# A two-layer trunk on one core: norm sums from one tile of squares, turned tiles split straight out of PSUM, and the last halves scaled and stored by two engines

## The chip, the cores and the metric

The kernel runs on one core of a Trainium2 chip. The metric is the device time of one execution in microseconds, the median over several runs. The engines are named as in the profile: PE (TensorE, matmul), PEld (its weight load), DVE (VectorE), ACT (ScalarE), POOL (GpSimd) and SP (SyncE, which here only issues DMAs).

## What is computed

The reference is a decoder trunk of two layers over 512 tokens of width 1024, in float32. Layer 0 mixes with a gated convolution and a pooling over several window sizes, layer 1 with a gated position mixing; each layer then has a gated feed-forward net of hidden width 2816, and a norm closes the trunk.

```python
def rms_norm(x, g):
    y = x * rsqrt(mean(x * x, axis=-1) + EPS)
    return y * g

def reference(x, ...):
    h = x
    # layer 0
    proj = rms_norm(h, norm_mix[0]) @ w_in_even          # a_b, a_c, a_v, z_b: 512 columns each
    y_a = a_b * causal_dwconv3(a_c * a_v, conv_a)
    y_b = multiscale_pool(z_b, w_pool, pool_scale)       # windows 2, 4, 8, 16
    h = h + concat(y_a, y_b) @ w_out_even
    h = h + gated_conv_ffn(rms_norm(h, norm_ffn[0]), ...)
    # layer 1
    ...                                                  # mixer C
    h = h + gated_conv_ffn(rms_norm(h, norm_ffn[1]), ...)
    return rms_norm(h, final_norm)
```

## The kernel before

**Layout.** The residual `h` lies in SBUF with the features on the partitions: eight tiles `h[k]` of 128 features by 512 tokens. A product in float32 is made of three fast matmuls: each operand is split into a high part, rounded to the fast format, and a low part that holds the rest (`hi` and `lo`), and `mm3` adds hi x hi (L139), lo x hi (L140) and hi x lo (L141) into one PSUM bank. So each tile of weights and of activations passes through ScalarE, which writes `hi`, and VectorE, which subtracts it from the raw value to get `lo`. For weights `parts` does this (`whi` at L134, `wlo` at L135).

**The norm** is not applied to the activations ahead of a product. The products use `h` times the gain, split into `hgh` and `hgl`, and the results are scaled by the reciprocal root of each token's mean square later. Class `Norm` collects the squares: ScalarE squares `h[k]`, GpSimd adds the squares into one tile `ssq` (L195). With `apart=True`, which norms m0 (first mixer), f0 and f1 (the two feed-forward nets) use, the eighth square is not added but kept in a tile `last`. `rstd_tokens` then sums over the partitions on TensorE, with two matmuls of one column for each of four tiles of tokens, one on `ssq` (L203) and one on `last` (L204): eight in all, into `sst`. `inv_sqrt_cols` makes the reciprocal root out of it with a square root on ScalarE (L233) and one Newton step in small VectorE operations; `rstd_spread` turns the result into a tile over all tokens (`ssr`, L211, and a copy at L214).

**The z stage** opens the kernel. `x` comes with the tokens on the partitions, so for each k TensorE turns four 128 x 128 blocks into a PSUM bank `xt_ps` (L363). From there, in `turn(k)`:

```python
inorder(nc.scalar.activation(whi, wraw, AF.Copy))                      # L371
inorder(nc.vector.tensor_copy(h[k], ps))                               # L372
inorder(nc.scalar.activation(hg[k][0], h[k], AF.Copy, scale=g))        # L374
inorder(nc.vector.tensor_tensor(wlo, wraw, ..., ALU.subtract))         # L375
inorder(nc.vector.scalar_tensor_tensor(hg[k][1], h[k], g, hg[k][0]))   # L376
norm.square(k, inorder)                                                # L188, L191, L194
```

`turn(k + 1)` is called when the group `z` begins its products of k. `in_group("z", ...)` then adds 12 matmuls of 128 x 512 per k into four banks. At the end of its first bank `z_done` starts the norm's sums, at the third it spreads the root and starts the pooling of VectorE (`z_pool`).

**Behind it** follow the groups `ac`, `av`, the pooled product (its weights `wpl` are split by two instructions at the end of the z stage's code) and `ab`, each with four splits of weights of 128 x 1024, and then the output projection. The raw weights come through one SP queue with four buffers; `whi` and `wlo` have six.

**Order.** A scheduler places the instructions of each engine by priorities and estimated times. `inorder` keeps marked instructions in the order of the program among themselves; `behind(a, b)` puts instruction a after b in the order, without a semaphore.

**The feed-forward nets** begin with `direct`, which calls `first(i, j)` ahead of each product of three matmuls; at `(1, 0)` it calls `rstd_tokens`, at `(2, 2)` `rstd_spread`.

**The end.** The last product of the second net is finished for four tiles of tokens, each in two halves of 512 columns: VectorE adds the residual, ScalarE squares with a running sum, `newton` gives the root's parts, and VectorE scales both halves (L950) with two factors at once, `r` and `ms`; SP stores each half (L952).

Of the kernel before, what the change touches and what calls it, by code (L numbers as in the profile page):

```python
# [8 lines left out]
F32 = mybir.dt.float32  # L9
# [6 lines left out]
P = 128  # L16
D = 1024
S = 512
# [12 lines left out]
def tile_trunk(ctx: ExitStack, tc: tile.TileContext, x, norm_mix, norm_ffn, final_norm,  # L31
# [96 lines left out]
        nc.scalar.activation(hi, raw, AF.Copy)  # L128
        return hi, lo

    def parts(raw, a, b, name):
        hi = wp.tile([P, a, b], F32R, tag="whi", bufs=6, name=f"whi_{name}")
        lo = wp.tile([P, a, b], F32R, tag="wlo", bufs=6, name=f"wlo_{name}")
        nc.scalar.activation(hi, raw, AF.Copy)  # L134
        nc.vector.tensor_tensor(lo, raw, hi.bitcast(F32), ALU.subtract)  # L135
        return hi, lo

    def mm3(ps, lhs, rhs, start, stop):
# [33 lines left out]
    class Norm:  # L172


        def __init__(self, name, gain, apart=False):
            self.name, self.gain, self.n, self.apart = name, gain, 0, apart
            self.ssq = tp.tile([P, S], F32, tag="ssq", bufs=1, name=f"ssq_{name}")

        def add(self, k):
# [3 lines left out]
                                           op0=ALU.mult, op1=ALU.subtract)  # L183
            self.square(k)

        def square(self, k, order=lambda ins: ins):
            if self.n == 0:
                order(nc.scalar.activation(self.ssq, h[k], AF.Square))  # L188
            elif self.n == NK - 1 and self.apart:
                self.last = tp.tile([P, S], F32, tag="rstd", name=f"last_{self.name}")  # L190
                order(nc.scalar.activation(self.last, h[k], AF.Square))  # L191
            else:
                sq = tp.tile([P, S], F32, tag="sq", name=f"sq_{self.name}{k}")
                order(nc.scalar.activation(sq, h[k], AF.Square))  # L194
                nc.gpsimd.tensor_tensor(self.ssq, self.ssq, sq, ALU.add)  # L195
            self.n += 1

        def rstd_tokens(self):

            ps = aux_bank(f"sst_{self.name}")  # L200
            for t in range(NT):
                ts_ = slice(t * P, (t + 1) * P)
                nc.tensor.matmul(ps[:, t : t + 1], self.ssq[:, ts_], ones, start=True, stop=False)  # L203
                nc.tensor.matmul(ps[:, t : t + 1], self.last[:, ts_], ones, start=False, stop=True)  # L204
            self.cols = inv_sqrt_cols(ps[:, :NT], NT, f"{self.name}t")

        def rstd_spread(self):

            ps = aux_bank(f"ssr_{self.name}")
            for t in range(NT):  # L210
                nc.tensor.transpose(ps[:, t * P : (t + 1) * P],  # L211
                                    self.cols[:, t : t + 1].to_broadcast([P, P]), ident)
# [4 lines left out]
        def rstd_cols(self):  # L217
            ps = aux_bank(f"ssc_{self.name}")
            for t in range(NT):
                nc.tensor.matmul(ps[:, t : t + 1], self.ssq[:, t * P : (t + 1) * P],  # L220
                                 ones, start=True, stop=True)
            return inv_sqrt_cols(ps[:, :NT], NT, f"{self.name}c")

    def work(key, n, name):
        if n == S:
# [86 lines left out]
    def in_parts(chunks, k, raw):  # L312
        hi, lo = parts(*raw)
        for i in range(raw[1]):
            chunks[k + i] = hi[:, i, :], lo[:, i, :]

    def in_group(name, w, c0, lhs_is_weight, on_done, tail, chunks=None, before=None):
        if chunks is None:
            chunks = {}
            for k in range(0, NK, 2):  # L320
                in_parts(chunks, k, in_fetch(name, w, c0, k, 2))
# [12 lines left out]
        if lhs_is_weight:  # L334
            group(name, range(4), list(range(NK)), wt, lambda k, j: hg_k(k), tail, on_done, before)
        else:
            group(name, range(4), list(range(NK)), tokens, wt_wide, tail, on_done, before)

    def mixer0():
        nonlocal prm0  # L340
        w = w_in_even[0]
        with tc.tile_pool(name="m0", bufs=1) as mp:
            prm_mix = params("mix", [("mix", rows_of(norm_mix[0]), NK)], nc.scalar)
            norm = Norm("m0", lambda k: prm_mix("mix", k), apart=True)
            zchunks = {}
            xt = {}

# [6 lines left out]
                raws[k] = in_fetch("z", w, 1536, k, n)  # L354

            raws = {}
            for k, n in ((0, 1), (1, 1), (2, 2), (4, 2)):
                load(k, n)

            def turn(k):  # L360
                ps = mm_bank(f"xt_ps{k}")
                for t in range(NT):
                    nc.tensor.transpose(ps[:, t * P : (t + 1) * P], xt[k][:, t, :], ident)  # L363
# [7 lines left out]
                inorder(nc.scalar.activation(whi, wraw, AF.Copy))  # L371
                inorder(nc.vector.tensor_copy(h[k], ps))  # L372
                g = prm_mix("mix", k)
                inorder(nc.scalar.activation(hg[k][0], h[k], AF.Copy, scale=g))  # L374
                inorder(nc.vector.tensor_tensor(wlo, wraw, whi.bitcast(F32), ALU.subtract))  # L375
                inorder(nc.vector.scalar_tensor_tensor(  # L376
                    hg[k][1], h[k], g, hg[k][0].bitcast(F32), op0=ALU.mult, op1=ALU.subtract))
                norm.square(k, inorder)
                if k == 0:
                    load(6, 2)  # L380

# [16 lines left out]

            def z_done(g, ps):
                if g == 0:  # L400
                    norm.rstd_tokens()
# [70 lines left out]

            in_group("ab", w, 0, True, b_done, 4)

            nxt = Norm("f0", lambda k: prm0("ffn", k), apart=True)
            project("oe", w_out_even[0], mix, [4, 5, 6, 7, 0, 1, 2, 3], nxt)
            return nxt

# [15 lines left out]
    class Ffn:  # L494
# [262 lines left out]
    def mixer1(norm):  # L757
        w = w_in_odd[0]
        with tc.tile_pool(name="m1", bufs=1) as mp:
# [113 lines left out]
                    for j in ((4,), (5,), (6, 7))[k - 1]:  # L873
                        turned(j)

            nxt = Norm("f1", lambda k: prm1("ffn", k), apart=True)
            project("oo", w_out_odd[0], mix, list(range(NK)), nxt, before=second_half)
            return nxt

# [1 line left out]
    def ffn1(norm):  # L881
        with tc.tile_pool(name="f1", bufs=1) as ap:
# [20 lines left out]
            for groups, a, b in PARTS:  # L903
# [24 lines left out]
                def done(j, ps):  # L928
# [18 lines left out]
                    nc.vector.tensor_scalar(ms, ms, 1.5, None, op0=ALU.add)  # L947
                    for c in range(2):
                        cs = slice(c * 512, (c + 1) * 512)
                        nc.vector.tensor_scalar(y[t][:, cs], yf[c], r, ms,  # L950
                                                op0=ALU.mult, op1=ALU.mult)
# [50 lines left out]
```

## Time and profile before

| | us |
|---|---|
| median of three runs | 1000.65 (1000.1 to 1001.06) |
| the profiled execution | 1000.02 |
| its span on the core | 998.3 |
| TensorE busy | 986.5 (99%) |
| VectorE, ScalarE, GpSimd busy | 699.9, 522.7, 100.6 |

The mean clock that TensorE was granted is 0.998. Rows of the timeline that are shown below read: start in us from the span's start, duration in us, engine, line, operation, output <- inputs, their shapes, how many instructions the row joins, and in brackets the engine's idle time before it with what ended it. Successive records of one engine overlap by up to a tenth of a microsecond. Rows of the waits read: engine, waiting output and line, what it waited for, and then total us, count and the longest.

### The profile page before, as it was taken

The page shows a single profiled execution, that of the slowest core. Times are in us where ns is not written, and L with a number is a line of the kernel's source. Part 1 is how long each engine was busy: PE and PEld are TensorE (multiplying, and loading weights), DVE is VectorE, ACT ScalarE, POOL GpSimd, SP SyncE. Part 2 cuts the span into 40 slices and gives each one's busy share as a digit, 9 for nine tenths or more (in the row PEclk, how much of TensorE's full clock was granted, in tenths as well). Part 3 has the DMA queues.
Part 4 walks back from the last instruction along what each step waited for, and adds up shares of the span by engine and source line. Part 5 has one row for each costly group of instructions (what it writes and reads, how often), then busy time and mean ns, then how long its engine had stood idle before and what let it go on. Part 6 is the DMA issues. An engine that isn't in the chain of part 4 may idle for free.

```text
span 998.3 us, 14727 instructions
## 1 busy us (share of the span) xinstructions
PE 986.5 (99%) x5835; PEld 874.5 (88%) x5835; DVE 699.9 (70%) x1057; ACT 522.7 (52%) x775; POOL 100.6 (10%) x117
## 2 busy tenths in 40 slices
PE   8999999999999999999999999999999999999997
PEld 6888888898999989999888888888989899898995
DVE  5977457967785877858943645389668868688677
ACT  6522345744653746537655444675536366363663
POOL 3032030300000000000300001202000010000100
PEclk9999999999999999999999999999999999999999
DMA  7532225454554645546433223434535446354442
GB/s 233 184 105 85 85 85 127 107 150 124 130 145 106 175 121 132 144 106 184 132 127 106 63 86 104 100 91 118 158 95 145 141 112 184 94 141 146 119 115 84
DMA packets 81904, 124.53 MB, mean 125 GB/s; under 512 B 4292, under 2 KB 53676, under 8 KB 81836
## 3 DMA queue, kind: packets, MB, share of 16 engines
q1 hardware_dynamic: 73580, 98.96, 31.6%
q0 software_dynamic: 6912, 23.07, 12.9%
q10 hardware_dynamic: 1344, 1.58, 0.5%
q8 instruction: 45, 0.74, 0.3%
q14 instruction: 23, 0.19, 0.1%
HBM read 98.42 MB, written 2.10 MB: 101 GB/s over the span
## 4 chain that ended last, share of the span: by engine, by line
PE 92%; DVE 4%; DMA 2%; ACT 1%; issue 0%; SPq 0%; POOL 0%; DVEq 0%; ACTq 0%; POOLq 0%
PE d L139 4%; PE d L140 4%; PE d L141 4%; PE dn L139 4%; PE dn L140 3%; PE dn L141 3%; PE gu L139 3%; PE gu L141 3%; PE gu L140 3%; PE u L141 1%; PE oo L141 1%; PE oo L139 1%; PE u L140 1%; PE u L139 1%; PE oe L140 1%; PE oe L139 1%
## 5 line engine op out<-in xcount | busy, mean ns | idle before, releaser
L139 PE MATMUL dn<-whi_dn,a_hi 128*128 128x512 f32 x176 | 68.7, 390 | 0.0
L140 PE MATMUL d<-a_lo,whi_d 128*128 128x512 f32 x176 | 68.6, 390 | 0.0
L140 PE MATMUL dn<-wlo_dn,a_hi 128*128 128x512 f32 x176 | 68.6, 390 | 0.0
L141 PE MATMUL d<-a_hi,wlo_d 128*128 128x512 f32 x176 | 68.5, 389 | 0.0
L514 DVE SCALAR_TENSOR_TENSOR c<-rows,prm,c 128x512 f32<-128x512 f32 x88 | 67.5, 791 | 0.0
L141 PE MATMUL dn<-whi_dn,a_lo 128*128 128x512 f32 x176 | 67.3, 390 | 0.0
L139 PE MATMUL d<-a_hi,whi_d 128*128 128x512 f32 x176 | 66.9, 390 | 0.0
L127 POOL DMA_DIRECT2D wlo_g<-raw_g x22 | 19.1, 868 | 382.3 <-ACT wlo_g L126 350.7
L931 DVE TENSOR_TENSOR y<-dn,y 128x512 f32<-128x512 f32 x48 | 32.3, 685 | 22.8 <-PE dn L141 22.3
L126 ACT ACTIVATE wlo_g<-raw_g 128x1024 fp32r<-128x1024 f32 x22 | 23.2, 1055 | 42.4 <-PE dn L140 42.4
L135 DVE TENSOR_TENSOR wlo_u<-raw_u,whi_u 128x1024 fp32r<-128x1024 f32 x16 | 19.6, 1223 | 34.2 <-ACT whi_u L134 34.1
L520 ACT ACTIVATE s<-c,prm 128x512 f32<-128x512 f32 x44 | 30.9, 717 | 22.7 <-DVE c L514 22.6
L640 ACT ACTIVATE whi_s12u<-s12u 128x1024 fp32r<-128x1024 f32 x18 | 18.9, 1050 | 43.1 <-PE d L140 33.7
L641 DVE TENSOR_TENSOR wlo_s34u<-s34u,whi_s34u 128x1024 fp32r<-128x1024 f32 x18 | 22.1, 1226 | 26.1 <-ACT whi_s34u L640 26.1
L141 PEld LDWEIGHTS dn<-whi_dn,a_lo 128*128 128x128 f32 x176 | 33.0, 188 | 7.5 <-DVE a_lo L255 0.2
L140 PEld LDWEIGHTS d<-a_lo,whi_d 128*128 128x128 f32 x176 | 33.1, 188 | 7.2 <-DVE a_lo L255 0.2
L139 PEld LDWEIGHTS dn<-whi_dn,a_hi 128*128 128x128 f32 x176 | 33.1, 188 | 7.1 <-ACT a_hi L253 0.2
L139 PEld LDWEIGHTS d<-a_hi,whi_d 128*128 128x128 f32 x176 | 32.8, 188 | 7.0
L298 DVE TENSOR_TENSOR h<-d,h 128x512 f32<-128x512 f32 x48 | 32.5, 685 | 9.2 <-PE d L141 9.2
L141 PEld LDWEIGHTS d<-a_hi,wlo_d 128*128 128x128 f32 x176 | 33.0, 188 | 6.7
L140 PEld LDWEIGHTS dn<-wlo_dn,a_hi 128*128 128x128 f32 x176 | 33.1, 188 | 6.5
L135 DVE TENSOR_TENSOR wlo_dn<-raw_dn,whi_dn 128x1024 fp32r<-128x1024 f32 x22 | 26.8, 1221 | 12.8 <-ACT whi_dn L134 12.8
(1201 smaller groups left out, 3412.3 us busy)
## 6 DMA issues: line engine op xcount, KB each, us to landing
raw_g<-in_w_ffn_gate_dram SPq DMA_DIRECT2D x36, 512.0 KB, 4.0
raw_u<-in_w_ffn_up_dram SPq DMA_DIRECT2D x36, 512.0 KB, 4.0
wlo_g<-raw_g POOLq DMA_DIRECT2D x22, 512.0 KB, 4.8
raw_d<-in_w_ffn_down_dram SPq DMA_DIRECT2D x22, 512.0 KB, 4.4
raw_dn<-in_w_ffn_down_dram SPq DMA_DIRECT2D x22, 512.0 KB, 4.7
wlo_u<-raw_u POOLq DMA_DIRECT2D x18, 512.0 KB, 4.7
raw_oe<-in_w_out_even_dram SPq DMA_DIRECT2D x8, 512.0 KB, 3.5
raw_g<-in_w_ffn_gate_dram SPq DMA_DIRECT2D x16, 256.0 KB, 2.9
```

The lines of the kernel that those rows point to most:

```text
L126: nc.scalar.activation(lo, raw, AF.Copy, scale=-1.0)
L127: nc.gpsimd.dma_start(lo, raw, accum_op=ALU.add)
L135: nc.vector.tensor_tensor(lo, raw, hi.bitcast(F32), ALU.subtract)
L139: nc.tensor.matmul(ps, lhs[0], rhs[0], start=start, stop=False)
L140: nc.tensor.matmul(ps, lhs[0], rhs[1], start=False, stop=False)
L141: nc.tensor.matmul(ps, lhs[1], rhs[0], start=False, stop=stop)
L298: nc.vector.tensor_tensor(h[k], ps, h[k], ALU.add)
L514: nc.vector.scalar_tensor_tensor(c, t[:, i : S + i], prm("cf", i * NF + ft), c, op0=ALU.mult, op1=ALU.add)
L520: nc.scalar.activation(s, c, AF.Silu, bias=self.prm("bf", ft))
L640: nc.scalar.activation(hi, src, AF.Copy)
L641: nc.vector.tensor_tensor(lo, src, hi.bitcast(F32), ALU.subtract)
L931: nc.vector.tensor_tensor(dst, ps, dst, ALU.add)
```

## The change

- **Norm.** `apart` and `rstd_tokens` are gone. All eight squares go into `ssq` by way of GpSimd, and `rstd_cols` sums it with four matmuls of one column (`ssc`). In the feed-forward nets it is called at `(1, 2)`, the spread at `(2, 1)`, both kept in the order of the program.
- **z stage.** `hgh`, `hgl` and the square read the turned tile in PSUM; `h[k]` is still copied, after `hgl`. VectorE's order for a k is wlo, hgl, copy. The splits of `wpl` and of the four `ac` weights are put behind the last square (ScalarE) and the last hgl (VectorE) of the stage.
- **End.** The Newton step is written out so that one factor `r` comes out; VectorE scales the low half and SP stores it, ScalarE scales the high half and stores it through its own queue.

```diff
-    def parts(raw, a, b, name):
+    def parts(raw, a, b, name, after=(None, None)):
...
-        nc.scalar.activation(hi, raw, AF.Copy)
-        nc.vector.tensor_tensor(lo, raw, hi.bitcast(F32), ALU.subtract)
+        behind(nc.scalar.activation(hi, raw, AF.Copy), after[1])
+        behind(nc.vector.tensor_tensor(lo, raw, hi.bitcast(F32), ALU.subtract), after[0])
...
-        def square(self, k, order=lambda ins: ins):
+        def square(self, k, order=lambda ins: ins, src=None):
+            src = h[k] if src is None else src
             if self.n == 0:
-                order(nc.scalar.activation(self.ssq, h[k], AF.Square))
-            elif self.n == NK - 1 and self.apart:
-                self.last = tp.tile([P, S], F32, tag="rstd", name=f"last_{self.name}")
-                order(nc.scalar.activation(self.last, h[k], AF.Square))
+                order(nc.scalar.activation(self.ssq, src, AF.Square))
             else:
...
-        def rstd_tokens(self):
-            ps = aux_bank(f"sst_{self.name}")
-            for t in range(NT):
-                ts_ = slice(t * P, (t + 1) * P)
-                nc.tensor.matmul(ps[:, t : t + 1], self.ssq[:, ts_], ones, start=True, stop=False)
-                nc.tensor.matmul(ps[:, t : t + 1], self.last[:, ts_], ones, start=False, stop=True)
-            self.cols = inv_sqrt_cols(ps[:, :NT], NT, f"{self.name}t")
...
+        def rstd_cols(self, order=lambda ins: ins):
             ps = aux_bank(f"ssc_{self.name}")
             for t in range(NT):
-                nc.tensor.matmul(ps[:, t : t + 1], self.ssq[:, t * P : (t + 1) * P],
-                                 ones, start=True, stop=True)
-            return inv_sqrt_cols(ps[:, :NT], NT, f"{self.name}c")
+                order(nc.tensor.matmul(ps[:, t : t + 1], self.ssq[:, t * P : (t + 1) * P],
+                                       ones, start=True, stop=True))
+            self.cols = inv_sqrt_cols(ps[:, :NT], NT, f"{self.name}c")
+            return self.cols
...
+            fed = [None, None]
+            def put_square(ins):
+                fed[1] = inorder(ins)
...
                 inorder(nc.scalar.activation(whi, wraw, AF.Copy))
+                g = prm_mix("mix", k)
+                inorder(nc.scalar.activation(hg[k][0], ps, AF.Copy, scale=g))
+                inorder(nc.vector.tensor_tensor(wlo, wraw, whi.bitcast(F32), ALU.subtract))
+                fed[0] = inorder(nc.vector.scalar_tensor_tensor(
+                    hg[k][1], ps, g, hg[k][0].bitcast(F32), op0=ALU.mult, op1=ALU.subtract))
                 inorder(nc.vector.tensor_copy(h[k], ps))
-                g = prm_mix("mix", k)
-                inorder(nc.scalar.activation(hg[k][0], h[k], AF.Copy, scale=g))
-                inorder(nc.vector.tensor_tensor(wlo, wraw, whi.bitcast(F32), ALU.subtract))
-                inorder(nc.vector.scalar_tensor_tensor(
-                    hg[k][1], h[k], g, hg[k][0].bitcast(F32), op0=ALU.mult, op1=ALU.subtract))
-                norm.square(k, inorder)
+                norm.square(k, put_square, ps)
...
-            nc.scalar.activation(wpl_hi, wpl, AF.Copy)
-            nc.vector.tensor_tensor(wpl_lo, wpl, wpl_hi.bitcast(F32), ALU.subtract)
+            behind(nc.scalar.activation(wpl_hi, wpl, AF.Copy), fed[1])
+            behind(nc.vector.tensor_tensor(wpl_lo, wpl, wpl_hi.bitcast(F32), ALU.subtract), fed[0])
...
-            in_group("ac", w, 512, True, c_done, 4)
+            in_group("ac", w, 512, True, c_done, 4, after=fed)
...
-                    if (i, j) == (1, 0):
-                        self.norm.rstd_tokens()
-                    elif (i, j) == (2, 2):
-                        self.r = self.norm.rstd_spread()
+                    if (i, j) == (1, 2):
+                        self.norm.rstd_cols(inorder)
+                    elif (i, j) == (2, 1):
+                        self.r = self.norm.rstd_spread(inorder)
...
-                    newton(ms, 1, f"fin{t}", r)
-                    nc.vector.tensor_scalar(ms, ms, 1.5, None, op0=ALU.add)
-                    for c in range(2):
-                        cs = slice(c * 512, (c + 1) * 512)
-                        nc.vector.tensor_scalar(y[t][:, cs], yf[c], r, ms,
-                                                op0=ALU.mult, op1=ALU.mult)
-                        nc.sync.dma_start(out[t * P : (t + 1) * P, cs], y[t][:, cs])
+                    sd = work("sd", 1, f"fin{t}")
+                    nc.scalar.activation(sd, ms, AF.Sqrt)
+                    nc.vector.reciprocal(r, sd)
+                    nc.vector.scalar_tensor_tensor(ms, ms, r, r, op0=ALU.mult, op1=ALU.mult)
+                    nc.vector.tensor_scalar(ms, ms, -0.5, 1.5, op0=ALU.mult, op1=ALU.add)
+                    nc.vector.tensor_tensor(r, r, ms, ALU.mult)
+                    lo, hi = (y[t][:, c * 512 : (c + 1) * 512] for c in range(2))
+                    nc.vector.tensor_scalar(lo, yf[0], r, None, op0=ALU.mult)
+                    nc.scalar.activation(hi, yf[1], AF.Copy, scale=r)
+                    nc.sync.dma_start(out[t * P : (t + 1) * P, :512], lo)
+                    nc.scalar.dma_start(out[t * P : (t + 1) * P, 512:], hi)
```

More of the change, by code (lines that the diff above doesn't have):

```diff
@@ L172, in tile_trunk, with __init__ @@
     class Norm:
-        def __init__(self, name, gain, apart=False):
-            self.name, self.gain, self.n, self.apart = name, gain, 0, apart
+        def __init__(self, name, gain):
+            self.name, self.gain, self.n = name, gain, 0
             self.ssq = tp.tile([P, S], F32, tag="ssq", bufs=1, name=f"ssq_{name}")
@@ L184, in add, with rstd_spread @@
             self.square(k)
-        def square(self, k, order=lambda ins: ins):
+        def square(self, k, order=lambda ins: ins, src=None):
+            src = h[k] if src is None else src
             if self.n == 0:
-                order(nc.scalar.activation(self.ssq, h[k], AF.Square))
-            elif self.n == NK - 1 and self.apart:
-                self.last = tp.tile([P, S], F32, tag="rstd", name=f"last_{self.name}")
-                order(nc.scalar.activation(self.last, h[k], AF.Square))
+                order(nc.scalar.activation(self.ssq, src, AF.Square))
             else:
                 sq = tp.tile([P, S], F32, tag="sq", name=f"sq_{self.name}{k}")
-                order(nc.scalar.activation(sq, h[k], AF.Square))
+                order(nc.scalar.activation(sq, src, AF.Square))
                 nc.gpsimd.tensor_tensor(self.ssq, self.ssq, sq, ALU.add)
             self.n += 1
-        def rstd_tokens(self):
-            ps = aux_bank(f"sst_{self.name}")
-            for t in range(NT):
-                ts_ = slice(t * P, (t + 1) * P)
-                nc.tensor.matmul(ps[:, t : t + 1], self.ssq[:, ts_], ones, start=True, stop=False)
-                nc.tensor.matmul(ps[:, t : t + 1], self.last[:, ts_], ones, start=False, stop=True)
-            self.cols = inv_sqrt_cols(ps[:, :NT], NT, f"{self.name}t")
-        def rstd_spread(self):
+        def rstd_spread(self, order=lambda ins: ins):
             ps = aux_bank(f"ssr_{self.name}")
             for t in range(NT):
-                nc.tensor.transpose(ps[:, t * P : (t + 1) * P],
-                                    self.cols[:, t : t + 1].to_broadcast([P, P]), ident)
+                order(nc.tensor.transpose(ps[:, t * P : (t + 1) * P],
+                                          self.cols[:, t : t + 1].to_broadcast([P, P]), ident))
             r = tp.tile([P, S], F32, tag="rstd", name=f"rstd_{self.name}")
@@ L215, in rstd_spread @@
             return r
-        def rstd_cols(self):
+        def rstd_cols(self, order=lambda ins: ins):
             ps = aux_bank(f"ssc_{self.name}")
             for t in range(NT):
-                nc.tensor.matmul(ps[:, t : t + 1], self.ssq[:, t * P : (t + 1) * P],
-                                 ones, start=True, stop=True)
-            return inv_sqrt_cols(ps[:, :NT], NT, f"{self.name}c")
+                order(nc.tensor.matmul(ps[:, t : t + 1], self.ssq[:, t * P : (t + 1) * P],
+                                       ones, start=True, stop=True))
+            self.cols = inv_sqrt_cols(ps[:, :NT], NT, f"{self.name}c")
+            return self.cols
     def work(key, n, name):
@@ L310, in in_fetch, with in_parts, in_group @@
                      n, 512, f"{name}_{k}")
-    def in_parts(chunks, k, raw):
-        hi, lo = parts(*raw)
+    def in_parts(chunks, k, raw, after=(None, None)):
+        hi, lo = parts(*raw, after=after)
         for i in range(raw[1]):
             chunks[k + i] = hi[:, i, :], lo[:, i, :]
-    def in_group(name, w, c0, lhs_is_weight, on_done, tail, chunks=None, before=None):
+    def in_group(name, w, c0, lhs_is_weight, on_done, tail, chunks=None, before=None,
+                 after=(None, None)):
         if chunks is None:
@@ L320, in in_group @@
             for k in range(0, NK, 2):
-                in_parts(chunks, k, in_fetch(name, w, c0, k, 2))
+                in_parts(chunks, k, in_fetch(name, w, c0, k, 2), after)
         def wt(k, j):
@@ L343, in mixer0 @@
             prm_mix = params("mix", [("mix", rows_of(norm_mix[0]), NK)], nc.scalar)
-            norm = Norm("m0", lambda k: prm_mix("mix", k), apart=True)
+            norm = Norm("m0", lambda k: prm_mix("mix", k))
             zchunks = {}
@@ L400, in z_done @@
                 if g == 0:
-                    norm.rstd_tokens()
+                    norm.rstd_cols()
                 elif g == 2:
@@ L473, in mixer0 @@
             in_group("ab", w, 0, True, b_done, 4)
-            nxt = Norm("f0", lambda k: prm0("ffn", k), apart=True)
+            nxt = Norm("f0", lambda k: prm0("ffn", k))
             project("oe", w_out_even[0], mix, [4, 5, 6, 7, 0, 1, 2, 3], nxt)
@@ L874, in second_half @@
                         turned(j)
-            nxt = Norm("f1", lambda k: prm1("ffn", k), apart=True)
+            nxt = Norm("f1", lambda k: prm1("ffn", k))
             project("oo", w_out_odd[0], mix, list(range(NK)), nxt, before=second_half)
```

## The prediction

> **What bounds the kernel now.** I read the page's busy shares and chain first, then the waits of TensorE.
>
> ```profile
> span 998.3 us, 14727 instructions
> PE 986.5 (99%) x5835; PEld 874.5 (88%) x5835; DVE 699.9 (70%) x1057; ACT 522.7 (52%) x775; POOL 100.6 (10%) x117
> PE 92%; DVE 4%; DMA 2%; ACT 1%; issue 0%; SPq 0%; POOL 0%; DVEq 0%; ACTq 0%; POOLq 0%
> PE xt_ps L363 <- DMA xt<-in_x_dram: 1.2, 1, 1.2
> PE z L140 <- DVE hgl L376: 1.1, 2, 0.8
> ```
>
> The span is matmul from end to end: PE is busy 986.5 of 998.3 us, and of its waits the only ones near the change are 1.2 us for the first x tiles and 1.1 us for two hgl tiles. An edit can therefore pay in three ways only: fewer matmuls, no wait in the z stage, a shorter tail. It can cost by making TensorE wait where it does not wait now.
>
> **The z stage: the loop around one k.** Before, TensorE sets the pace; the timeline of two ks:
>
> ```profile
> 10.20 0.60 PE L363 MATMUL xt_ps<-ident,xt 128*128 128x128 f32 x4
> 11.56 0.72 ACT L374 ACTIVATE hgh<-h,prmmix 128x512 fp32r<-128x512 f32 x1 [0.28 <-DVE h L372]
> 12.19 0.62 ACT L194 ACTIVATE sq_m<-h 128x512 f32<-128x512 f32 x1
> 12.71 0.62 ACT L371 ACTIVATE whi_z<-raw_z 128x512 fp32r<-128x512 f32 x1
> 12.95 1.28 POOL L195 TENSOR_TENSOR ssq_m<-ssq_m,sq_m 128x512 f32<-128x512 f32 x1 [1.71 <-ACT sq_m L194]
> 13.40 0.60 PE L363 MATMUL xt_ps<-ident,xt 128*128 128x128 f32 x4
> ```
>
> The turned tiles of successive ks stand 13.40 - 10.20 = 3.20 us apart. In the changed kernel hgh, hgl, the copy of h and the square all read the same PSUM bank. VectorE's order becomes wlo, hgl, copy, and in the built program the square of a k waits for VectorE's copy of that k. ScalarE's order is whi, hgh, square, so whi of the next k stands behind that square. That is a loop over two engines; its length is decided by a third, GpSimd, as a later stretch of the same trace shows:
>
> ```profile
> 20.99 1.29 POOL L195 TENSOR_TENSOR ssq_m<-ssq_m,sq_m 128x512 f32<-128x512 f32 x1 [3.55 <-ACT sq_m L194]
> 21.02 0.68 DVE L372 COPY h<-xt_ps 128x512 f32<-128x512 f32 x1
> 21.63 1.19 DVE L375 TENSOR_TENSOR wlo_z<-raw_z,whi_z 128x512 fp32r<-128x512 f32 x1
> 22.74 0.74 DVE L376 SCALAR_TENSOR_TENSOR hgl<-h,prmmix,hgh 128x512 fp32r<-128x512 f32 x1
> 23.13 1.51 POOL L195 TENSOR_TENSOR ssq_m<-ssq_m,sq_m 128x512 f32<-128x512 f32 x1 [0.85 <-ACT sq_m L194]
> 26.68 1.34 POOL L195 TENSOR_TENSOR ssq_m<-ssq_m,sq_m 128x512 f32<-128x512 f32 x1 [2.04 <-ACT sq_m L194]
> 26.79 1.78 DVE L376 SCALAR_TENSOR_TENSOR hgl<-h,prmmix,hgh 128x512 fp32r<-128x512 f32 x1
> 11.44 0.68 DVE L375 TENSOR_TENSOR wlo_z<-raw_z,whi_z 128x512 fp32r<-128x512 f32 x1
> ```
>
> A VectorE operation with both inputs in SBUF does not run while GpSimd adds. wlo, 0.68 us at 11.44, takes 1.19 at 21.63 and ends at 22.82, 0.54 after the add's end at 22.28; hgl at 26.79 takes 1.78 and ends at 28.57, 0.55 after the add's end at 28.02. The copy out of PSUM at 21.02 lies inside the same add and keeps its 0.68. Before, most adds fall where VectorE has nothing of that kind to do. In the change each add starts as the square ends (12.81 to 12.95: 0.14 later), while the next wlo can start only after whi: ScalarE's next instruction starts 0.10 ahead of a record's end (12.71 against 12.81), so whi ends about 0.53 after that same square. So every wlo meets an add already running. The loop: 0.14 to the add, 1.29 for it, 0.54 until wlo ends, minus 0.08 because VectorE's next instruction starts 0.08 ahead of the record's end (22.82 against 22.74), hgl 0.74 less the same 0.08 = 0.66, the copy 0.69, 0.03 to the square (next fence: 6.40 to 6.43), the square 0.62. Sum 3.89 us against TensorE's 3.20. The change removes a copy from the chain to hgl, but makes a longer loop that now sets the pace.
>
> The Trainium skill's page "SBUF — State Buffer", section "SBUF: two separate sides", calls the port pair that VectorE shares with GpSimd an exclusive lock, held for a whole instruction, and counts among those that need it a VectorE operation with two SBUF inputs against a GpSimd one that reads SBUF. The trace agrees on the exclusion (1.19 for 0.68), but by the page's "fully blocks" wlo would need its whole 0.68 after the add instead of the measured 0.54, 0.14 more in each of six loops, and my sum would be 0.8 higher.
>
> **Where the loop begins and what it delays.**
>
> ```profile
> 5.01 0.66 PE L363 MATMUL xt_ps<-ident,xt 128*128 128x128 f32 x4
> 5.61 0.63 ACT L371 ACTIVATE whi_z<-raw_z 128x512 fp32r<-128x512 f32 x1 [2.67 <-DMA raw_z<-in_w_in_even_dram]
> 5.71 0.69 DVE L372 COPY h<-xt_ps 128x512 f32<-128x512 f32 x1 [0.42 <-PE xt_ps L363]
> 6.43 0.72 ACT L374 ACTIVATE hgh<-h,prmmix 128x512 fp32r<-128x512 f32 x1 [0.19 <-DVE h L372]
> 30.97 0.62 ACT L191 ACTIVATE last_m<-h 128x512 f32<-128x512 f32 x1
> 31.49 1.04 ACT L134 ACTIVATE whi_ac<-raw_ac 128x1024 fp32r<-128x1024 f32 x1
> 33.21 0.36 PE L204 MATMUL sst_m<-small,last_m 128*128 128x1 f32 x2
> 33.61 0.17 DVE L241 TENSOR_SCALAR ms_m0t<-sst_m 128x4 f32<-128x4 f32 x1 [0.90 <-PE sst_m L204]
> 33.80 0.20 ACT L233 ACTIVATE sd_m0t<-ms_m0t 128x4 f32<-128x4 f32 x1 [1.27 <-DVE ms_m0t L241]
> 33.98 0.39 PE L139 MATMUL ac<-hgh,whi_ac 128*128 128x512 f32 x1
> 34.21 0.40 PE L140 MATMUL ac<-hgl,whi_ac 128*128 128x512 f32 x1
> 52.37 1.22 DVE L135 TENSOR_TENSOR wlo_av<-raw_av,whi_av 128x1024 fp32r<-128x1024 f32 x1
> 58.16 0.39 PE L139 MATMUL av<-hgh,whi_av 128*128 128x512 f32 x1
> ```
>
> With these durations and overlaps, k=0: whi from 5.61 (its tile is turned by 5.67), hgh directly behind it 6.15 to 6.87, hgl 6.90 to 7.64, copy 7.56 to 8.25, square 8.28 to 8.90. This first square goes into ssq itself, without an add. k=1: whi 8.80 to 9.43, hgh 9.34 to 10.06, wlo 9.46 to 10.14, hgl 10.09 to 10.83, copy 10.75 to 11.44, square 11.47 to 12.09. Six loops of 3.89 more: the eighth square ends at 12.09 + 23.34 = 35.43, where last_m now ends at 31.59.
>
> Behind it stands all that leads to the next stage, since the four whi_ac (1.04 each), which now run inside the z stage, are put behind the squares and come behind the norm's square root in ScalarE's order: add 35.57 to 36.86; four sums on TensorE, 0.85 (next part), to 37.71; ms 0.04 + 0.17 and root 0.02 + 0.20 (the spacings at 33.57 to 34.00), to 38.14; whi_ac from 38.04 to 39.08; the first ac matmul at about 39.2 (0.1 for the handing over, my estimate between the 0.03 and 0.14 seen above). TensorE has only two z matmuls of about 0.23 (33.98 to 34.21) left after the sums, so it waits here about a microsecond. From the first ac matmul to the first av one it is 58.16 - 33.98 = 24.18 us now, 8 z matmuls (1.84) among them, which in the change all come earlier: 22.34. First av at 39.2 + 22.34 = 61.54: **3.4 us later**. The matmuls that m0 loses are inside this figure.
>
> Does VectorE then hold av back? Three wlo_ac of about 1.14 and wpl_lo of 0.6 move behind the z stage, some 4 us, and the stage itself ends 5.2 later. The last wlo_av ends at 53.59 now and would end near 62.8; but that is the part for the last two ks, which TensorE reaches 54 matmuls (12 us) after 61.54, and the fourth wlo_ac, the only one of its group placed behind pooling work, is likewise needed 54 matmuls after 39.2. I count nothing. The five parameter loads that SP now issues ahead of the last av load feed nothing earlier than that.
>
> The end of the loop is uncertain on both sides. Were wlo to take only the 1.19 of 21.63 from its own start, each loop loses 0.19, six lose 1.1. Were every add to take the 1.51 of 23.13, six gain 1.3. So the front lies between +2.3 and +4.7; I take 3.4, made from the commonest durations.
>
> **The norms of f0 and f1.**
>
> ```profile
> 149.79 0.62 ACT L191 ACTIVATE last_f<-h 128x512 f32<-128x512 f32 x1
> 149.92 0.75 DVE L182 SCALAR_TENSOR_TENSOR hgl<-h,prm,hgh 128x512 fp32r<-128x512 f32 x1 [1.10 <-ACT hgh L181]
> 150.65 0.28 PE L203 MATMUL sst_f<-small,ssq_f 128*128 128x1 f32 x2
> 152.35 0.49 PE L139 MATMUL gu<-hgh,whi_g 128*128 128x512 f32 x1
> 643.04 0.28 PE L203 MATMUL sst_f<-small,ssq_f 128*128 128x1 f32 x2
> 644.74 0.48 PE L139 MATMUL gu<-hgh,whi_g 128*128 128x512 f32 x1
> ```
>
> Eight narrow sums hold TensorE for 152.35 - 150.65 = 1.70 us, and as much at 643. Four take 0.85, so each norm saves 0.85 of pure matmul time: **-1.70**. The sums move six matmuls later, to 150.65 + 6 x 0.23 = 152.03, and the spread three earlier. The square now goes through GpSimd: ready at 150.41, the add waits for hgl at 149.92, which ends at 150.67, and at 1.29 ends at 151.96. That is less than 0.1 ahead of its use: just hidden.
>
> **The tail.**
>
> ```profile
> 993.54 0.15 DVE L947 TENSOR_SCALAR ssf<-ssf 128x1 f32<-128x1 f32 x1
> 993.73 1.00 DVE L950 TENSOR_SCALAR y<-yf,rc_fin,ssf 128x512 f32<-128x512 f32 x2
> ```
>
> The Newton step keeps its three small operations. The two halves took 1.00 on VectorE to 994.73; now ScalarE does the high half in the 0.72 of hgh at 11.56, from the same 993.73, to 994.45, a gain of 0.28 at best; nothing if the stores share what carries them, and up to 0.5 lost if ScalarE comes to its store late (one more such operation). I take **-0.15**.
>
> The page "DMA: Bandwidth & Descriptors" of the Trainium skill, section "Issuing engines are not separate DMA queues", says that issuing from two engines saves only the time of issuing. No run yet shows it for these stores; by it the second queue itself brings nothing and only the 0.28 counts.
>
> **Sum.** +3.4 - 1.70 - 0.15 = +1.55 us on the profiled 1000.02 (1.7 of it outside the span). The median of the runs is 1000.65, so the forecast is 1002.2.
>
> **Rivals.** *The loop stays at TensorE's pace* (chance 0.14). If wlo slips in ahead of the add, or the square does not in fact wait for the copy, the loop is 0.53 for whi, 0.03 + 0.60 for wlo, then 0.66, 0.69, 0.03 and 0.62 = 3.16, TensorE's 3.20 rules, and six times 0.69 = 4.1 us of the front go away: 1.55 - 4.1 = -2.55, 998.1. For it: the change takes the copy out of the path to hgl, where the two waits of 1.1 us lie. Against it: the add is ready 0.4 us before wlo in every k.
>
> *The add is late for f0's sums* (0.11), slower: their margin is under 0.1. GpSimd's last add meets VectorE's hgl, and if it then takes 1.51, or is held for one more VectorE operation of 0.75, TensorE waits 0.1 to 0.9, and in f1 alike if its squares end as close. It decides from the point where the add ends after 152.03. Midway, 0.7 more: +2.25, 1002.9.
>
> *The forecast* has 0.75. Within its bounds (+0.45 to +2.85, with the tail's from there +0.3 to +3.5) the border of 0.2% (2.0 us, about what a measurement of this kernel can tell from no change) lies a little above its likeliest value: 0.45 below it, 0.30 above.
>
> So faster 0.14, same 0.45, slower 0.30 + 0.11 = 0.41. The range starts from the forecast's bounds on the median, 1000.95 to 1004.15, which hold the second rival too; the low end goes 0.35 lower, since the runs of before lie up to half a microsecond around their median, and the high end 0.25 lower, since both upper bounds would have to meet: 1000.6 to 1003.9. The first rival is left out.
>
> **What would show it.** Right: in the changed trace the turned tiles of successive ks from the third on are 3.8 to 3.9 us apart, wlo_z takes 1.2 or more and ends 0.5 after an add, TensorE waits for whi_ac about 1 us, the first av matmul stands near 61.5; ssc takes 0.85 at f0 and f1. Wrong: ks 3.2 apart (the first rival), a wait at ssc_f (the second), or a wait in ac or av for a wlo. A first av near 58 or below would refute the main step.

## The result: slower by 0.38%, and the profile after

The changed kernel takes 1004.69 us (median of six runs, 1002.72 to 1005.74) against 1000.79 for the kernel before: a ratio of 1.0038, 95% interval 1.0025 to 1.0051, or 3.9 us. The forecast was 1002.2, no change clear of the measurement. The profiled execution took 1004.75, its span is 1003.0, 4.7 above the 998.3 before.

The busy line of the page and TensorE's waits, to set beside those of before (columns of the waits: total us, count, longest):

```profile
PE 988.2 (99%) x5811; PEld 872.9 (87%) x5811; DVE 701.7 (70%) x1053; ACT 523.7 (52%) x779; POOL 102.3 (10%) x120
PE z L140 <- DVE hgl L372: 2.4, 6, 0.5
PE ac L139 <- ACT whi_ac L134: 0.9, 1, 0.9
PE ssc_m L210 <- POOL ssq_m L193: 0.8, 1, 0.8
PE u_16b L628 <- DMA wlo_u<-raw_u: 0.4, 1, 0.4
```

TensorE has 24 matmul records fewer and is nevertheless busy 1.7 us longer. That already says that the idle times (2.4 + 0.9 + 0.8) are not all: some matmuls themselves ran slower. One turn of the z stage's loop, from the timeline:

```profile
20.07 0.62 ACT L368 ACTIVATE whi_z<-raw_z 128x512 fp32r<-128x512 f32 x1
20.32 1.29 POOL L193 TENSOR_TENSOR ssq_m<-ssq_m,sq_m 128x512 f32<-128x512 f32 x1 [2.64 <-ACT sq_m L192]
20.73 1.43 DVE L371 TENSOR_TENSOR wlo_z<-raw_z,whi_z 128x512 fp32r<-128x512 f32 x1 [1.24 <-ACT whi_z L368]
22.08 0.74 DVE L372 SCALAR_TENSOR_TENSOR hgl<-xt_ps,prmmix,hgh 128x512 fp32r<-128x512 f32 x1
22.74 0.67 DVE L374 COPY h<-xt_ps 128x512 f32<-128x512 f32 x1
23.51 0.60 ACT L192 ACTIVATE sq_m<-xt_ps 128x512 f32<-128x512 f32 x1 [2.23 <-DVE h L374]
24.25 1.29 POOL L193 TENSOR_TENSOR ssq_m<-ssq_m,sq_m 128x512 f32<-128x512 f32 x1 [2.64 <-ACT sq_m L192]
21.57 0.60 PE L360 MATMUL xt_ps<-ident,xt 128*128 128x128 f32 x4
25.54 0.60 PE L360 MATMUL xt_ps<-ident,xt 128*128 128x128 f32 x4
```

From add to add it is 24.25 - 20.32 = 3.93 us, of 3.89 forecast, and the turned tiles stand 3.97 apart here. wlo begins inside the add and ends at 22.16, 0.55 after the add's end at 21.61. The end of the stage, and the first matmuls of ac:

```profile
35.31 0.60 ACT L192 ACTIVATE sq_m<-xt_ps 128x512 f32<-128x512 f32 x1 [2.24 <-DVE h L374]
37.38 1.05 PE L210 MATMUL ssc_m<-small,ssq_m 128*128 128x1 f32 x8 [0.82 <-POOL ssq_m L193]
38.78 3.89 ACT L134 ACTIVATE whi_ac<-raw_ac 128x1024 fp32r<-128x1024 f32 x4
39.87 0.52 PE L139 MATMUL ac<-hgh,whi_ac 128*128 128x512 f32 x1 [0.87 <-ACT whi_ac L134]
41.04 0.63 PE L140 MATMUL ac<-hgl,whi_ac 128*128 128x512 f32 x1
41.47 0.63 PE L139 MATMUL ac<-hgh,whi_ac 128*128 128x512 f32 x1
63.97 0.39 PE L139 MATMUL av<-hgh,whi_av 128*128 128x512 f32 x1
```

The first ac matmul is at 39.87 (forecast 39.2). But from there to the first av one it is 24.10 us, not 22.34, and successive ac matmuls stand 0.43 apart instead of 0.23. The windows name the reason (columns: window, length, busy time of PE, PEld, DVE, ACT, POOL with counts, granted TensorE clock, DMA share, GB/s):

```profile
36.00:38.00 2.00, 1.18 (x9) 0.74 (x7) 0.00 (x0) 1.40 (x3) 1.27 (x1) 1.00 0.41 144
38.00:40.00 2.00, 1.13 (x7) 0.70 (x8) 1.33 (x6) 1.33 (x3) 0.00 (x0) 1.00 0.00 0
40.00:42.00 2.00, 2.00 (x6) 1.57 (x7) 2.00 (x3) 2.00 (x3) 0.00 (x0) 0.55 0.00 0
42.00:44.00 2.00, 2.00 (x9) 1.65 (x8) 1.42 (x2) 1.25 (x2) 0.00 (x0) 0.59 0.80 241
44.00:46.00 2.00, 2.00 (x11) 1.60 (x10) 1.97 (x4) 1.06 (x1) 0.00 (x0) 1.00 0.76 263
```

After four microseconds in which TensorE was busy 2.31, its clock was halved for 3.4 us, from 40.2 to 43.6. Over 40 to 44 the granted clock is 0.57 on the mean, so 43% of four microseconds was lost: 1.7 us. The prediction has no such term.

The norm of f0 and the tail:

```profile
156.36 1.29 POOL L193 TENSOR_TENSOR ssq_f<-ssq_f,sq_f 128x512 f32<-128x512 f32 x1 [0.81 <-ACT sq_f L192]
157.81 0.95 PE L210 MATMUL ssc_f<-small,ssq_f 128*128 128x1 f32 x8
158.62 0.48 PE L139 MATMUL gu<-hgh,whi_u 128*128 128x512 f32 x1
998.47 0.48 DVE L950 TENSOR_SCALAR y<-yf,rc_fin 128x512 f32<-128x512 f32 x1
998.53 0.72 ACT L951 ACTIVATE y<-yf,rc_fin 128x512 f32<-128x512 f32 x1 [0.93 <-DVE rc_fin L948]
```

The four sums hold TensorE for 0.81 us instead of 1.70, and the add is done at 157.65, 0.16 ahead of them. In the tail the high half is ready at 999.25, 0.72 after its start; before, both halves together took 1.00.

### The profile page after: what moved, and what is told of

The parts are those of the page before. It is cut to its first block, busy times and chain, and to the rows that moved or that the text cites. A ratio compares the mean times of both kernels' runs of the same rounds, so it can differ in the third digit from the quotient of the medians.

```text
span 1003.0 us, 14682 instructions
## 1 busy us (share of the span) xinstructions
PE 988.2 (99%) x5811; PEld 872.9 (87%) x5811; DVE 701.7 (70%) x1053; ACT 523.7 (52%) x779; POOL 102.3 (10%) x120
## 4 chain that ended last, share of the span: by engine, by line
PE 91%; DVE 4%; DMA 2%; ACT 1%; issue 1%; POOL 0%; ACTq 0%; SPq 0%; POOLq 0%
PE dn L139 4%; PE dn L141 4%; PE dn L140 4%; PE d L139 4%; PE d L140 4%; PE d L141 4%; PE gu L139 3%; PE gu L141 3%; PE gu L140 3%; PE u L139 1%; PE oo L139 1%; PE u L141 1%; PE oo L141 1%; PE u L140 1%; PE oe L141 1%; PE oe L140 1%
## 5 line engine op out<-in xcount | busy, mean ns | idle before, releaser
L193 POOL TENSOR_TENSOR ssq_f<-ssq_f,sq_f 128x512 f32<-128x512 f32 x14 | 18.9, 1347 | 181.6 <-ACT sq_f L192 146.7
```

## The experiments

Each kernel was timed in one of three sets, beside the kernel before, whose medians there were 1000.74 (first set: whi ahead, the first whi_ac, the first filling, the first norms and tail), 1001.32 (second: no adds, the change again, the second filling, the first kernel with all waits out) and 1001.08 (third: the rest). Times of different sets are best compared by what they differ from the kernel before.

### whi ahead of the square

```diff
 # in turn(k), the changed kernel; chunk(k) rounds whi_z of k on ScalarE
-                inorder(nc.scalar.activation(whi, wraw, AF.Copy))
...
+                if k < NK - 1:
+                    chunk(k + 1)
                 norm.square(k, put_square, ps)
```

> The changed kernel with one move: ScalarE rounds whi_z of k+1 ahead of the square of k instead of behind it. Theory A (the loop over wlo, hgl, copy, square and the next whi, stretched by GpSimd's add, sets the z stage's pace): wlo of k+1 is ready to run before the add starts, the turned tiles of successive ks stand 3.2 to 3.3 us apart instead of 3.93, first av near 57 to 58 instead of 64.0, no stretch of halved TensorE clock before it; 997.5 to 998.5 us, below the kernel before. Theory B (the front is late because the splits of ac are put behind the stage, whatever its pace): ks 3.2 apart but a wait for whi_ac of 1 us or more remains and the clock halves again: 1000 to 1001. Theory C (two readers of one PSUM bank are what costs): pace still near 3.9, about 1004.5.

Measured: 999.26 us, ratio 0.9986 (0.9977 to 0.9995): 5.4 below the change, 1.5 below the kernel before, and 0.8 above the range that theory A gave. The timeline, turned tiles, wlo and add:

```profile
17.00 0.60 PE L370 MATMUL xt_ps<-ident,xt 128*128 128x128 f32 x4
20.21 0.60 PE L370 MATMUL xt_ps<-ident,xt 128*128 128x128 f32 x4
19.69 0.68 DVE L376 TENSOR_TENSOR wlo_z<-raw_z,whi_z 128x512 fp32r<-128x512 f32 x1
20.60 1.29 POOL L193 TENSOR_TENSOR ssq_m<-ssq_m,sq_m 128x512 f32<-128x512 f32 x1 [1.35 <-ACT sq_m L192]
56.96 0.39 PE L139 MATMUL av<-hgh,whi_av 128*128 128x512 f32 x1
```

wlo now runs ahead of the add and takes 0.68; the pace is TensorE's 3.21; the first av matmul comes 7.0 earlier than in the change, at a clock of 1.00 throughout. Theory A holds in the trace; its time was too low, and the profile shows 1.3 us of waits in the nets (see the norms and the tail below). Theory B asked for a remaining wait for whi_ac of 1 us, of which there is none, since ten z matmuls now lie behind the sums. Theory C is excluded: the same engines still read the same PSUM banks.

### No adds

```diff
-                nc.gpsimd.tensor_tensor(self.ssq, self.ssq, sq, ALU.add)
+                if self.name != "m0" or self.n == NK - 1:
+                    nc.gpsimd.tensor_tensor(self.ssq, self.ssq, sq, ALU.add)
```

This kernel leaves out six of the adds, so its first norm sums two squares only and its output is not that of the trunk; it serves for the timing alone.

> The changed kernel without GpSimd's adds for k = 1 to 6 of the first norm (left out, so that this norm's sum is of two squares only); the order on all engines stays. Theory A (the add holds back wlo, 1.43 instead of 0.68): wlo takes 0.68, the turned tiles stand about 3.2 apart, first av near 58 (near 59.6 with a halved clock): 998.8 to 1000.5. Rival (the square waiting for the copy is enough by itself for a slower pace): ks stay above 3.6 apart and the time above 1002.5.

Measured: 1000.12 us, ratio 0.9990 (0.9981 to 0.9999). Timeline and one window:

```profile
19.99 0.60 PE L361 MATMUL xt_ps<-ident,xt 128*128 128x128 f32 x4
23.20 0.60 PE L361 MATMUL xt_ps<-ident,xt 128*128 128x128 f32 x4
22.23 0.69 DVE L372 TENSOR_TENSOR wlo_z<-raw_z,whi_z 128x512 fp32r<-128x512 f32 x1 [1.24 <-ACT whi_z L369]
36.00:38.00 2.00, 2.00 (x9) 1.61 (x7) 2.00 (x4) 1.96 (x3) 0.00 (x0) 0.51 0.19 32
```

The order on all engines is that of the change, the square still waits for the copy and whi for the square. With the adds gone wlo takes 0.69 and the pace is 3.21. So the loop alone would have kept up; it is GpSimd's add on top of wlo that stretches it, 0.74 us in each k. The two waits at the stage's end stayed (0.6 and 0.9), and the clock was halved behind them here too, from 36.0 to 39.4 us.

### The first whi_ac ahead of the root

```diff
+        if name == "ac_0":          # in parts(): the square root of m0 behind this whi
+            behind(marks["m0c"], ins)
```

> The changed kernel with ScalarE rounding the first whi_ac ahead of the norm's square root instead of behind it. The z stage keeps its 3.93 us per k. The wait of 0.87 us of the first ac matmul goes, the wait of 0.82 for GpSimd's last add stays. If the halved clock of 3 us that follows comes from TensorE's idle time adding up over the end of the stage, it may go too: 1004.7 - 0.9 - 1.6 = 1002.2; if the 0.82 alone is enough, or the idle time inside the stage, the halving stays: 1003.8.

Measured: 1002.38 us, ratio 1.0017 (1.0008 to 1.0025). That is 1.6 above before, where the change is 3.9 above in its first measurement and 2.9 in its second (see the next experiment): 1.3 to 2.3 us are gained, of which the wait itself is 0.9. The wait that is left, and the windows after the stage, which have their clock back:

```profile
36.87 1.05 PE L215 MATMUL ssc_m<-small,ssq_m 128*128 128x1 f32 x8 [0.80 <-POOL ssq_m L198]
38.00:40.00 2.00, 1.96 (x9) 1.26 (x8) 2.00 (x5) 1.84 (x3) 0.00 (x0) 1.00 0.00 0
40.00:42.00 2.00, 2.00 (x9) 1.63 (x10) 2.00 (x3) 1.21 (x2) 0.00 (x0) 1.00 0.44 133
```

Here the wait of 0.8 for the add alone did not halve the clock. This is one profile, and its start differs: the clock is halved from 8.0 to 11.5 us, behind a wait of 1.5 for the x tiles, and the z stage then has three waits for hgl instead of six. That halving at the start comes and goes.

### The waits filled

Seven matmuls whose results are overwritten, three ahead of the sums and four ahead of the first ac matmul, with all else in its place:

```diff
+                one = filler(banks[j], 3, z[0])          # behind the last hi x hi of z
+                behind(marks["ssc"][0], one)
...
+                two = filler(banks[j], 4, z[1])          # ahead of ac's first matmul
```

> The changed kernel with seven extra matmuls of 128x512, whose results are overwritten, in the two waits at the end of the z stage (three ahead of the norm's sums, four ahead of the first ac matmul), so that TensorE stays busy there and nothing else moves. If the halved clock follows from TensorE standing idle there, it stays at 1.00 and the time falls by 1.6 to 1.7: about 1003.0. If the halving has another cause (the switch of matmul kinds, the load of the other engines), it stays and the time is 1004.7 or more.

> The kernel with the filled waits again, with more runs: its first median lay only 0.8 below the change, while its profiled span lay 1.7 below, with no halved clock. If the halving after the stage is what the filling takes away, the median falls 1.6 below the change's of this set, less as often as the change itself runs without it.

Measured: 1003.88 (6 runs, ratio 1.0031, 1.0020 to 1.0043) and 1002.82 (11 runs, 1.0017, 1.0008 to 1.0026). The change itself, again, beside the second:

> The changed kernel once more, unaltered, beside the others of this set: about 1004.7. Its profile shows whether the halved clock after the z stage (40.4 to 43.4 us in the first profile) is there each time, or, as at the start of two other profiles (8 to 11.8 us), comes and goes.

Measured: 1004.24 (1.0030, 1.0020 to 1.0041). Timeline of the second filled kernel with one window, and then two rows and four windows of the change's second profile:

```profile
38.84 1.09 PE L151 MATMUL ac<-hgh 128*128 128x512 f32 x4
39.86 0.50 PE L144 MATMUL ac<-hgh,whi_ac 128*128 128x512 f32 x1
62.35 0.39 PE L144 MATMUL av<-hgh,whi_av 128*128 128x512 f32 x1
40.00:42.00 2.00, 2.00 (x12) 1.65 (x13) 2.00 (x2) 1.92 (x3) 0.00 (x0) 1.00 0.00 0
```

```profile
38.21 0.40 PE L141 MATMUL z<-hgh,wlo_z 128*128 128x512 f32 x1
39.47 0.79 PE L139 MATMUL ac<-hgh,whi_ac 128*128 128x512 f32 x1 [0.86 <-ACT whi_ac L134]
38.00:40.00 2.00, 1.14 (x4) 0.67 (x4) 1.73 (x6) 1.74 (x3) 0.00 (x0) 0.67 0.00 0
40.00:42.00 2.00, 2.00 (x6) 1.54 (x5) 2.00 (x4) 2.00 (x3) 0.00 (x0) 0.50 0.13 11
42.00:44.00 2.00, 2.00 (x8) 1.61 (x7) 1.11 (x2) 0.84 (x2) 0.00 (x0) 0.50 0.91 297
44.00:46.00 2.00, 2.00 (x8) 1.56 (x7) 2.00 (x4) 1.06 (x1) 0.00 (x0) 0.63 0.82 279
```

This is the cleanest pair. With the filling, the first ac matmul stands at 39.86, to 0.01 us where it stands in the change's first profile (the first whi_z of both starts alike, at 6.03 and 6.04); the clock stays at 1.00 and the first av one is at 62.35 instead of 63.97, 1.62 earlier, for nothing but matmuls that compute nothing. By the medians of the second set the filling is worth 1.4, by the first 0.8; each alone lies within the scatter. Taken together, with each set's kernel before taken off, 14 runs of the change and 17 of the filled kernel differ by 1.4 us, 0.2 to 2.7 by resampling the runs.

In its second profile the change paid for twice as long, from 38.7 to 45.5 us. Leaving out the end of the kernel, where TensorE has no more work, the fourteen profiles have five halved stretches; they last 3.4, 6.8, 3.4, 3.4 and 3.4 us: one length, or twice it. And the second one began at 38.7, when the wait for whi_ac had only just begun (the last z matmul ends at 38.61): by then TensorE had stood idle for 0.9 of the last 3.4 us, nearly all of it the wait for the add. So one wait of 0.8 was enough in this profile and not in that of the kernel with the first whi_ac ahead of the root. The fourteen runs of the change reach from 1002.08 to 1006.67; how much of that is the halving was not measured, since only two of them have a trace.

### The norms and the tail alone

The z stage, the first norm and the unplaced splits of before, with the changed f0 and f1 norms and the changed tail (the parts of the diff quoted for them, and no others).

> The kernel before with the changed norms of f0 and f1 and the changed tail, the z stage and the first norm as before. If the two norms save 0.85 each and the tail 0.1, and nothing else came with them: before minus 1.8, about 998.9 to 999.0 us, and the whole loss of the change lies in the z stage. If the norms bring a wait, no gain.

> The old z stage with the changed norms of f0 and f1 and the changed tail again, with new runs: by the sum 1.8 us under before; by the first measurement 1.0 (its profile had a start at half clock and a late wst, which cost that profile 1.6 and 1.2).

Measured: 999.73 (0.9994, 0.9985 to 1.0002) and 1000.04 (0.9989, 0.9980 to 0.9998), so 1.0 below before in both sets, the first time not clear of the scatter, where the sum gives 1.8. The kernel before, again:

> The kernel before once more, unaltered: ratio 1.000 within 0.1%. Its profile is a second one of the kernel before: if the waits of 0.3 to 1.3 us of u_16b and u_12b for a DMA, which all profiles with the changed norms but one show and the first profile of before does not, are there too, they are nothing that the norms brought; if they are absent again, the shorter norms give part of their 1.7 us back there.

Measured: ratio 1.0003 (0.9994 to 1.0012). TensorE's wait in the second profile of the kernel with norms and tail, which neither profile of before has:

```profile
PE u_16b L634 <- DMA wlo_u<-raw_u: 0.6, 1, 0.6
```

Eleven of the twelve profiles with the shorter norms wait 0.3 to 1.5 us in all at such products of the second half of each net for a low part that a DMA makes. The issue stands 5.46 or 5.47 us ahead of u_16b in the first net throughout, so nothing was issued later; the data land later, with both profiles of before in time. By these waits about half a microsecond of the norms' gain goes there; no run takes them away to show it. Why the landing moved was not tried and stays open.

### All waits out

The kernel with whi ahead, with the sums six matmuls later and the first whi_ac ahead of the root:

```diff
+            if name == "z" and (i, j) == (len(ks) - 2, 3):
+                behind(marks["ssc"][0], marks["mm"])
```

> As the kernel with whi_z ahead of the square, and two waits more taken away: the first norm's sums stand six matmuls later, behind the last bank's products of the next to last k, and the first whi_ac stands ahead of the square root. The wait of 0.71 us for GpSimd's last add goes: 0.7 below the kernel with whi_z ahead alone, about 998.5 and 2.2 below before. If the wait comes back as one for whi_ac or for the root, no gain.

> The version with whi_z ahead of the square, the sums later and the first whi_ac ahead of the root, again, beside the next one: about 998.0, 3 us under before (front 2.2 under before's, norms 1.7).

Measured: 998.0 (0.9968, 0.9956 to 0.9979) and 996.57 (0.9959, 0.9945 to 0.9972), the fastest here: 3.3 and 4.5 below before. Its first timeline:

```profile
31.98 0.95 PE L217 MATMUL ssc_m<-small,ssq_m 128*128 128x1 f32 x8
33.59 0.40 PE L144 MATMUL ac<-hgh,whi_ac 128*128 128x512 f32 x1
56.04 0.39 PE L144 MATMUL av<-hgh,whi_av 128*128 128x512 f32 x1
```

No idle time stands in brackets: between 8 and 56 us TensorE waits for nothing (the waits for the x tiles at the start and those in the nets are still there), and av comes at 56.04, 2.1 earlier than before the change.

### The start filled as well

```diff
+                    for i in range(4):     # behind the first turned tile, ahead of the second
+                        ins = nc.tensor.matmul(fill, idle[:, :P], idle, start=True, stop=True)
```

> The same with four matmuls on zeros in the wait for the second x tiles at the start (1.0 to 1.5 us in the profiles). If that wait is what now and then brings a halved clock from 8 to 11.8 us, the slower runs of this kernel go and its median falls by some tenths, its scatter with it; if the halving depends on something else, no change, or 0.2 more where the x tiles come early.

Measured: 997.6 (0.9966, 0.9953 to 0.9978) beside 996.57 without the filling. No gain; five runs each do not show whether the slow start became rarer. Its one profile has no wait for the x tiles, but one of 1.7 us ahead of the product wst in layer 1, where all but one of the others have 0.5.

## Why the prediction was wrong

**The loop: right.** Add to add 3.93 us where 3.89 was forecast; wlo 1.43, ending 0.55 after the add; ks 3.8 to 4.0 apart from the fourth on. Two experiments that touch it in different ways (whi ahead of the square; no adds) both bring 3.21 back. On the rule of the Trainium skill weighed there ("SBUF — State Buffer", section "SBUF: two separate sides"): the exclusion is as the page has it, and the measured 0.55 after the recorded end of the add decides against its whole 0.68. One small sum is off: by the prediction's own terms a wlo of 1.19 from its own start shortens the loop by 0.22, not 0.19, so that the low bounds belong 0.2 lower; nothing here hangs on it.

**The wait behind it: right in kind and size.** 0.87 for whi_ac of "about a microsecond", and 0.82 ahead of the sums, which lay inside the path. The first ac matmul was at 39.87 instead of 39.2. Of these 0.67, 0.43 is the start (the first whi_z at 6.04 us against 5.61), a DMA that varied: the change's second profile starts at 5.65 and has its first ac matmul at 39.47. So about a quarter of a microsecond is the loop's.

**The failed step** is the sentence "From the first ac matmul to the first av one it is 58.16 - 33.98 = 24.18 us now ... 22.34". It carried a stretch with TensorE always busy over to a place behind two waits, and took the clock with it. The waits were priced at their own length alone; what they do to the matmuls after them was not priced. It measured 24.10, 1.76 us more, of which the clock is 1.6, shown by the filling (1.62 in the traces, 1.4 by all runs). With the clock kept at 1.00 the filled kernel needs 62.35 - 39.86 = 22.49 us, so the matmul count behind the 22.34 was right and the clock was the error. With the delay kept and the halving away, the filled kernel measured 3.1 and 1.5 above before in its two sets. The forecast's +1.55 lies at the low end of that; with the 1.0 that the norms and the tail gave, in place of 1.85, it would be +2.4, in the middle. The kernel with the first whi_ac ahead of the root measured 1002.4, but that is near the forecast by luck: it lacks a wait of 0.9 that the forecast contains.

The Trainium skill, page "TensorE: Matmul & The Clock Gate", Part 1, tells of a monitor that halves the clock after an idle window of about 3.4 us. No wait of that length lies here: the clock was halved after 3.4 us in which TensorE stood idle for 1.4 us (first profile), 0.9 (second) or 0.9 (no adds). It was not halved behind the 0.4 to 0.5 in each k of the z stage, behind 0.7 (whi ahead) or 0.8 (the first whi_ac) at the stage's end, or behind 1.4 at the start of three profiles. The two groups overlap, so the amount of idle time alone does not say when it happens, and the rest stays open.

**What is left over.** The median came out 2.5 us above the forecast. The halved clock makes about 1.4 of it and the norms and the tail, below, 0.8; the rest is within the scatter.

**The norms: right as matmul time** (0.89 and 0.89 us against 0.85), but by the medians norms and tail together gave 1.0 of 1.8, the second term of the sum that was mis-sized: the sum took for granted that a microsecond saved at f0 arrives at the end. The "just hidden" add was hidden, by 0.16.

**The tail: right.** From the end of TensorE's last record to the end of the span it is 7.39 before and 7.31 after, 0.08 less (forecast 0.15), where the span is given to 0.1 us.

**The rivals.** The first (TensorE's pace) is refuted for the change, but is what the kernel does when whi is moved. The second, the late add at f0, did not occur. What came true was not on the list: a short wait that slows the engine after it. The range ended at 1003.9, 0.8 under the result.

## What to carry to other kernels

A wait of the bounding engine costs its own length and may cost the clock behind it: where waits that add up to about a microsecond fall within a few microseconds, look at the granted clock in the windows after them, and price the change with a halved stretch as well (here 1.7 us). When one operand path is shortened, write down the whole ring of engines that one iteration goes round, with the engines that exclude each other, and compare it with the bound's pace; here moving one instruction ahead of another took the pace of the stage from 3.93 to 3.21 us and turned the same change from 3.9 us slower into 1.5 faster. Then remove the last waits one by one: the version without any at the end of the stage was the fastest.

## What was not expected of the hardware

- TensorE's clock fell to half around two waits of 0.8 and 0.9 us, in both profiles of the change (for 3.4 us in one and 6.8 in the other) and, with waits of 0.6 and 0.9, without the adds (3.4). In the second profile of the change it fell before the second wait had lasted 0.1 us. Behind one wait of 1.5 us at the start it fell in two profiles (3.4 us each) and did not in three others with 1.4 us.
- The same transfer, issued 5.47 us ahead of its use, came in time in both profiles of before and mostly 0.3 to 0.7 us too late in kernels whose TensorE work is the same from there back to the norm.
